# Trunk of two token mixers: product formed in place, one broadcast and the last scalings moved, one square root dropped, four splits held back

## The chip, the cores and the metric

The kernel runs on one core of one Trainium2 chip. The metric is the device time of one execution in microseconds (us), as the median of several executions. TensorE does the matrix products, VectorE and ScalarE the work on their results, GpSimd a few sums and all roots, and SyncE issues every DMA.

## What is computed

Two residual layers over 2048 positions of 1024 channels, float32. Layer 0 mixes tokens by a gated short convolution, layer 1 by causal window means; each is followed by a gated embedding, and one RMSNorm ends the trunk.

```python
def short_conv_mixer(h, w_in, w_conv, w_out):
    b_g, c_g, v, z = jnp.split(h @ w_in, 4, axis=-1)
    y = b_g * causal_conv3(c_g * v, w_conv)
    return (jax.nn.silu(z) * y) @ w_out
...
    h = x
    for i in range(DEPTH):
        hn = rmsnorm(h, norm_mix[i])
        h = h + (short_conv_mixer if i == 0 else pool_mixer)(hn, ...)
        gate = jax.nn.sigmoid(rmsnorm(h, ple_norm[i]) @ ple_w_gate[i])
        h = h + gate * (p[i] @ ple_w_proj[i])
    return rmsnorm(h, final_norm)
```

In the convolution mixer, c_g * v is called u in the kernel and in this text.

## The kernel before

Activations lie with channels on the 128 partitions and positions along the free axis, in four chunks of T = 512 positions; a first and a second pass (`sc` = 0, 1) take two chunks each. Weights come in granules of 128 x 1024. Every float32 value is split into a rounded part (ScalarE, L117 for weights, L304 and L310 for activations) and a rest (VectorE, L118, L305 and L311), and each product is three matmuls (L276 to L278); a granule of eight blocks against one chunk is 24 matmuls. The rounded weights lie in a ring of four buffers (`wring`), so a cast L117 waits until TensorE has read an older granule for the last time. PSUM has seven buffers for products and one for sums.

`mixer_a` goes through eight pairs (j = 0 to 7) of a "cv" and a "zb" step. The two chunks are multiplied together by Strassen's scheme with seven products, x11, x21, t2, t1, t3, x22 and t4, each of 12 matmuls, and three of its sums leave PSUM by a copy on ScalarE (L432) into a work tile of the pool `wk` (ten buffers). `added` (L435) makes a further tile of 512 columns. u is formed in L491 to L497 in another `wk` tile of 528 columns, whose first two columns hold the halo of the convolution.

Norms: `fin1` sums the squares across partitions on TensorE (`tot`, L344), takes the root on GpSimd (L355) and writes a diagonal `dg` (VectorE, L360); `fin2` broadcasts it with one matmul (`bc`, L365) and copies it to `rb` in SBUF (L367). A list `hooks` holds such calls; `dense_w` pops one after the 24 matmuls of a granule. In `gate`, a granule's product is scaled by `rb` (L775), passed through the sigmoid (L776), multiplied (L777) and added (L778); the square for the next norm is taken by L331 and added to `acc` (L334).

"The turn" is the end of the first pass: `gate` of layer 1 on chunk 1, then a `filler` (small products, copied out by L758) and the second pass's `mixer_a`. During both gates `ahead` lets one operand of the second pass be fetched from HBM (tile `n`, four buffers, shared with the embeddings that the gate fetches) and split, once for each k.

`gate_last` does the last gate in halves of 256 columns. After a half's last granule `finish` takes the half's norm (`fin_fast`, L369 to L386) and scales six of eight tiles on VectorE (L848), two on GpSimd (L846), and issues the output.

The program is written in one order; the compiler's scheduler then sets the order of the instructions on each engine from its own model of times, and each engine runs its list strictly in order. So a change of buffers or of a call's place can move instructions far from the lines that were edited.

Of the kernel before, what the change touches and what calls it, by code (L numbers as in the profile page):

```python
# [13 lines left out]
ALU = mybir.AluOpType  # L14
# [4 lines left out]
T = 512  # L19
# [30 lines left out]
def trunk_kernel(ctx: ExitStack, tc: tile.TileContext, xT, xN, pT, wts, par, out):  # L50
# [15 lines left out]
    def wtile():  # L66
        return wk.tile([P, 528], F32, tag="wk", name="wk")
# [365 lines left out]
        return c  # L433

    def added(ps, c):  # L435
        o = wtile()[:, :T]
        nc.vector.tensor_tensor(out=o, in0=ps, in1=c, op=ALU.add)  # L437
        return o

    def pair_steps(sc, i, X):  # L440

        pa, pb = psum(), psum()
        w = next_granule(("sum", (sc, i, 0)))
        product(pa, w, 0, X("x11"), True)
        product(pb, w, HK, X("x21"), True)
        c1 = copied(pa)
        m1 = added(pb, c1)
        yield
        w = next_granule(("sum", (sc, i, 1)))
        product(pa, w, HK, X("t2"), False)  # L450
        c2 = copied(pa)
        pc = psum()
        product(pc, w, 0, X("t1"), True)
        c5 = copied(pc)
        yield
        w = next_granule(("sum", (sc, i, 2)))
        product(pa, w, 0, X("t3"), False)
        n2 = added(pa, c5)
        product(pc, w, HK, X("x22"), False)
        m2 = added(pc, c2)  # L460
        w = next_granule(("sum", (sc, i, 3)))
        product(pa, w, 0, X("t4"), False)
        yield m1, m2, pa, n2
# [7 lines left out]
    def mixer_a(sc, X, Y, later):  # L471
        def steps(j, i):
            return pair_steps(sc, 2 * j + i, X)

        cv_steps = steps(0, 0)
        due = []
        for j in range(KT):
            zb_steps = steps(j, 1)
            if j == 0:
                next(cv_steps)  # L480
                next(zb_steps)
                look[0] = LOOK
                if sc == 0:
                    rb = list(row_stats(0))[-1]
                    rb2 = []
                    for t in range(2):
                        rb2.append(rbp.tile([P, T], F32, tag="rb", name="rb2"))
                        nc.scalar.activation(out=rb2[t], in_=rb[t], func=AF.Square)
            cs1, cs2, v1, v2 = pair_of(cv_steps)
            us = []  # L490
            for t, (c, v) in enumerate(((cs1, v1), (cs2, v2))):  # L491
                u = wtile()
                if sc == 0:
                    vec(c, c, rb2[t], ALU.mult)
                nc.gpsimd.tensor_copy(out=u[:, 0:2], in_=uh[:, j, :] if t == 0 else us[0][:, T:T + 2])
                nc.vector.tensor_tensor(out=u[:, 2:2 + T], in0=v, in1=c, op=ALU.mult)
                us.append(u)  # L497
            if sc == 0:
                nc.gpsimd.tensor_copy(out=uh[:, j, :], in_=us[1][:, T:T + 2])
            if j:  # L500
                next(zb_steps)
            next(zb_steps)
            cvs = []
            for u in us:
                cv = wtile()
                nc.scalar.activation(out=cv[:, :T], in_=u[:, 0:T], func=AF.Copy, scale=pcol(C_CONV + j))  # L506
                for t in (1, 2):
                    nc.vector.scalar_tensor_tensor(out=cv[:, :T], in0=u[:, t:t + T],  # L508
                                                   scalar=pcol(C_CONV + 8 * t + j),
                                                   in1=cv[:, :T], op0=ALU.mult, op1=ALU.add)  # L510
                cvs.append(cv)
            for args in due:
                Y.add(*args)
            due = []
            if j == KT - 1:
                Y.begin(later)
            z1, z2, b1, b2 = pair_of(zb_steps)
            if sc == 0 and FOLDS <= j + 1 < FOLDS + 4:
                fold(j + 1 - FOLDS)
            if j + 1 < KT:  # L520
                cv_steps = steps(j + 1, 0)
                next(cv_steps)
            for i in () if sc else ((), (0,), (1,), (2,), (3,), (4, 5), (6, 7), ())[j]:
                prepare_sums(*divmod(i, KT // 2))
            for t, (z, b) in enumerate(((z1, b1), (z2, b2))):
                cv = cvs[t][:, :T]
                if sc == 0:
                    vec(z, z, rb[t], ALU.mult)
                    vec(cv, cv, rb[t], ALU.mult)
                zs = wtile()[:, :T]  # L530
                nc.scalar.activation(out=zs, in_=z, func=AF.Sigmoid)
                nc.vector.tensor_tensor(out=zs, in0=z, in1=zs, op=ALU.mult)
                nc.vector.tensor_tensor(out=cv, in0=cv, in1=zs, op=ALU.mult)
                if j % 2 == t == 0:
                    yt = [acts.tile([P, 2, T], F32, tag="act", name="y") for _ in range(2)]
                nc.vector.tensor_tensor(out=yt[t][:, j % 2, :], in0=b, in1=cv, op=ALU.mult)
            if j % 2:
                due.append((j // 2, yt))
        for args in due:
            Y.add(*args)  # L540
# [26 lines left out]
    def vec(out, in0, in1, op):  # L567
        nc.vector.tensor_tensor(out=out, in0=in0, in1=in1, op=op)
# [145 lines left out]
    def mixer_out(layer, Y, src):  # L714
# [12 lines left out]
        for n, name in enumerate(OUT_NAMES):  # L727
# [16 lines left out]
                           "t3": (0, 2 * i + 1, True), "x21": (1, 2 * i, True), "t4": (1, 2 * i + 1, True)}[name])  # L744
            if name == "x21":
                s[0].fin1()
        s[0].fin2()
        return a, hs, s

    def ple_half(layer, ch, pt, wp, h):  # L750
# [66 lines left out]
        return [s.fin1, nop, last]  # L817

    def gate_last(layer, ch, a, hs, s_in):
        hooks.extend([s_in.fin1, s_in.fin2])  # L820
        pt = next_granule(("p", layer * NCH + ch))
        base = W_GATE[layer]
        half = T // 2
        ss = [Stat(half), Stat(half)]
        held, ws, wps = [], {}, {}
        seq = []
        for i in range(KT + LAG):
            if i < KT:
# [1 line left out]
            if i >= LAG:  # L830
                seq.append((i - LAG, 1))

        def finish(hf):
            c0, c1 = hf * half, (hf + 1) * half
            on_pool = (1, 3)
            for k in on_pool:
                nc.scalar.activation(out=hs[k][:, c0:c1], in_=hs[k][:, c0:c1], func=AF.Copy, scale=pcol(G_FIN + k))
            bc = ss[hf].fin_fast()
            rb = rbp.tile([P, T], F32, tag="rb", name="rb")
            nc.scalar.copy(out=rb[:, :half], in_=bc)  # L840
            for q in range(2):
                o = acts.tile([P, 4, half], F32, tag="act", name="o")
                for i in range(4):
# [12 lines left out]
        for k, hf in seq:  # L856
# [8 lines left out]
            for kk, h2, g_ps, p_ps in held:  # L865
                b0, b1 = h2 * half, (h2 + 1) * half
                gate_out(g_ps, p_ps, hs[kk], s_in.rb, b0, b1)
                ss[h2].add(hs[kk][:, b0:b1], nc.vector)
                if kk == KT - 1:
                    finish(h2)  # L870
            held = []


    warm = pst.tile([P, T], F32, tag="st", name="warm")
# [61 lines left out]
    for sc in range(2):  # L936
# [2 lines left out]
        mixer_a(sc, X, Y, xT[chs[1]])  # L939
        filler(*((0, 3) if sc else (1, 0)))  # L940
        a, hs, s = mixer_out(0, Y, xT[chs[0]])
        hooks.extend([s[1].fin1, nop, s[1].fin2])
        ab, ss = ([], []), []
        for t, ch in enumerate(chs):
            def after_gate(k):
# [8 lines left out]
        Y = Outputs(2 * sc + 1, (3, 2, 1, 0))  # L954
        mixer_b(ab, ss, Y, sc, nop if sc else between_b, h_dram[chs[1]])
        a, hs, s = mixer_out(1, Y, h_dram[chs[0]])
        hooks.extend([s[1].fin1, nop, s[1].fin2])
        if sc == 0:
            X = Operands(second_operand)

        def ahead(k):
            if sc == 0:
                X.ahead(1)

        for t, ch in enumerate(chs):
# [65 lines left out]
```

## Time and profile before

| | |
|---|---|
| median of three executions | 1821.08 us (1820.91 to 1826.33) |
| profiled execution, its own time | 1822.86 us |
| its span, first to last instruction | 1820.9 us |
| TensorE's mean granted clock | 0.991 of full speed |
| matmuls | 7998 |

A wait of an engine is given with what ended it ("<-" and the engine, tile and line of the instruction that released it). The time outside the span (1822.86 against 1820.9) is start and end of the execution.

### The profile page before, as it was taken

Reading aid. Unit: us, or ns where it says so; the run is one execution under the profiler, and the core shown is the slowest. Engines: PE = TensorE matmul, PEld = TensorE weight load, DVE = VectorE, ACT = ScalarE, POOL = GpSimd, SP = SyncE. Lnnn points to the kernel's source line nnn. Section 1 sums busy time; section 2 is a strip of 40 time slices with the busy share of each in tenths; the row PEclk is TensorE's granted clock in tenths of the full one; section 3 lists DMA queues with packets and bytes.
Section 4 is the critical chain, followed back from the end, with each engine's and each line's share of the span. In section 5 each row is a group of like instructions: output and inputs, shape, how many; then the busy total and the mean of one; then the engine's idle time right before and its main releaser. Section 6 shows DMA issues by size and latency. Waiting matters only on the chain.

```text
span 1820.9 us, 22137 instructions
## 1 busy us (share of the span) xinstructions
PE 1766.7 (97%) x7998; PEld 1457.0 (80%) x7998; DVE 1368.1 (75%) x1897; ACT 758.0 (42%) x1148; POOL 226.9 (12%) x217
## 2 busy tenths in 40 slices
PE   8899999999999999999989999999999999999996
PEld 6688888878788888887868788887878888888786
DVE  6887777987987778888876555557798766578865
ACT  6633333355654311455553333334555411145432
POOL 0100000001322000023210000000132200002310
PEclk9899999999999999999999999999999999999998
DMA  9455566895455556844673424347545522274421
GB/s 350 171 185 197 196 232 213 287 335 181 141 190 184 184 192 227 287 147 142 197 258 130 141 97 150 110 147 283 194 134 192 182 100 93 99 263 148 134 103 47
DMA packets 123934, 329.71 MB, mean 181 GB/s; under 512 B 13744, under 2 KB 15792, under 8 KB 123824
## 3 DMA queue, kind: packets, MB, share of 16 engines
q1 hardware_dynamic: 123824, 328.30, 52.0%
q8 instruction: 62, 1.02, 0.2%
q14 instruction: 48, 0.39, 0.1%
HBM read 230.73 MB, written 97.52 MB: 180 GB/s over the span
## 4 chain that ended last, share of the span: by engine, by line
PE 72%; DVE 14%; DMA 5%; issue 5%; ACT 3%; POOL 1%; SPq 0%; DVEq 0%; ACTq 0%; POOLq 0%
PE mm L276 24%; PE mm L277 24%; PE mm L278 24%; DVE w L118 3%; DVE act L305 2%; DVE act L311 2%; DMA raw<-in_wts_dram 2%; ACT w L117 2%; DMA n<-ndr 2%; DVE h L722 1%; POOL r L355 1%; DVE wk L777 1%; DVE h L808 1%; DVE dg L360 0%; DVE h L574 0%
## 5 line engine op out<-in xcount | busy, mean ns | idle before, releaser
L276 PE MATMUL mm<-act,w 128*128 128x512 f32 (+1 forms) x2432 | 932.6, 386 | 15.9 <-ACT wk L432 11.3
L277 PE MATMUL mm<-act,w 128*128 128x512 f32 (+1 forms) x2432 | 937.0, 385 | 5.9 <-DVE act L305 3.9
L278 PE MATMUL mm<-act,w 128*128 128x512 f32 (+1 forms) x2432 | 927.4, 385 | 0.5 <-DVE w L118 0.5
L276 PEld LDWEIGHTS mm<-act,w 128*128 128x128 f32 x2432 | 458.6, 189 | 115.8 <-ACT wk L432 16.9
L277 PEld LDWEIGHTS mm<-act,w 128*128 128x128 f32 x2432 | 458.2, 188 | 98.5 <-DVE act L305 5.8
L278 PEld LDWEIGHTS mm<-act,w 128*128 128x128 f32 x2432 | 458.1, 188 | 91.7 <-DVE w L118 1.0
L117 ACT CAST w<-raw 128x1024 fp32r<-128x1024 f32 (+1 forms) x291 | 289.2, 1002 | 525.4 <-PE mm L278 427.1
L118 DVE TENSOR_TENSOR w<-raw,w 128x1024 fp32r<-128x1024 f32 (+1 forms) x291 | 346.7, 1197 | 101.4 <-ACT w L117 98.5
L334 POOL TENSOR_TENSOR acc<-acc,wk 128x512 f32<-128x512 f32 x97 | 143.6, 1480 | 484.7 <-ACT wk L331 484.7
L437 DVE TENSOR_TENSOR wk<-mm,wk 128x512 f32<-128x512 f32 x96 | 66.1, 689 | 91.2 <-PE mm L278 87.2
L311 DVE SCALAR_TENSOR_TENSOR act<-h,par_sb,act 128x512 fp32r<-128x512 f32 x108 | 112.8, 1048 | 25.5 <-ACT act L310 24.8
L331 ACT ACTIVATE wk<-h 128x512 f32<-128x512 f32 (+1 forms) x119 | 71.2, 599 | 92.5 <-DVE h L778 92.5
L310 ACT ACTIVATE act<-h,par_sb 128x512 fp32r<-128x512 f32 x108 | 77.1, 719 | 75.9 <-DVE h L722 72.8
L722 DVE TENSOR_TENSOR h<-mm,h 128x512 f32<-128x512 f32 x112 | 76.0, 685 | 26.4 <-PE mm L278 24.2
L305 DVE TENSOR_TENSOR act<-n,act 128x512 fp32r<-128x512 f32 x112 | 78.9, 731 | 21.9 <-ACT act L304 21.9
L304 ACT CAST act<-n 128x512 fp32r<-128x512 f32 x112 | 65.8, 619 | 62.1 <-DMA n<-ydr 34.2
L432 ACT COPY wk<-mm 128x512 f32<-128x512 f32 x96 | 53.1, 589 | 84.2 <-PE mm L278 83.6
L508 DVE SCALAR_TENSOR_TENSOR wk<-wk,par_sb 128x512 f32<-128x512 f32 x64 | 44.1, 748 | 39.5 <-ACT wk L506 39.5
L692 DVE TENSOR_TENSOR wk<-wk 128x526 f32<-128x526 f32 (+5 forms) x80 | 55.5, 694 | 2.4
L276 PE MATMUL mm<-w 128*128 128x512 f32 (+1 forms) x144 | 48.8, 350 | 7.0 <-ACT wk L758 4.5
L776 ACT ACTIVATE wk<-wk 128x512 f32<-128x512 f32 (+1 forms) x72 | 41.3, 579 | 26.3 <-DVE wk L775 26.0
L707 ACT ACTIVATE wk<-wk 128x512 f32<-128x512 f32 x32 | 20.2, 631 | 76.8 <-DVE wk L705 76.7
(122 smaller groups left out, 1271.8 us busy)
## 6 DMA issues: line engine op xcount, KB each, us to landing
raw<-in_wts_dram SPq DMA_DIRECT2D x156, 512.0 KB, 3.4
n<-ydr SPq DMA_DIRECT2D x84, 256.0 KB, 4.5
ydr<-y SPq DMA_DIRECT2D x32, 512.0 KB, 2.9
raw<-in_wts_dram SPq DMA_DIRECT2D x64, 256.0 KB, 3.1
raw<-sdo SPq DMA_DIRECT2D x32, 512.0 KB, 5.6
raw<-sda SPq DMA_DIRECT2D x32, 512.0 KB, 3.9
pdr<-wk SPq DMA_DIRECT2D x56, 256.0 KB, 5.6
n<-pdr SPq DMA_DIRECT2D x56, 256.0 KB, 3.5
```

The costliest lines, as they stand in the source:

```text
L117: nc.scalar.copy(out=hi[:, c], in_=raw[:, c])
L118: eng.tensor_tensor(out=lo[:, c], in0=raw[:, c], in1=hi[:, c].bitcast(F32), op=ALU.subtract)
L276: nc.tensor.matmul(out=ps, lhsT=wh, rhs=ah, start=first, stop=False, skip_group_check=skip)
L277: nc.tensor.matmul(out=ps, lhsT=wh, rhs=al, start=False, stop=False, skip_group_check=skip)
L278: nc.tensor.matmul(out=ps, lhsT=wl, rhs=ah, start=False, stop=last, skip_group_check=skip)
L305: nc.vector.tensor_tensor(out=a[:, 1, :], in0=y, in1=a[:, 0, :].bitcast(F32), op=ALU.subtract)
L310: nc.scalar.activation(out=a[:, 0, :], in_=h, func=AF.Copy, scale=pcol(gcol))
L311: nc.vector.scalar_tensor_tensor(out=a[:, 1, :], in0=h, scalar=pcol(gcol), in1=a[:, 0, :].bitcast(F32), op0=ALU.mult, op1=ALU.subtract)
L331: nc.scalar.activation(out=sq, in_=h, func=AF.Square)
L334: (eng or nc.gpsimd).tensor_tensor(out=acc, in0=acc, in1=sq, op=ALU.add)
L437: nc.vector.tensor_tensor(out=o, in0=ps, in1=c, op=ALU.add)
L722: nc.vector.tensor_tensor(out=hs[t][k], in0=ps, in1=hs[t][k], op=ALU.add)
```

## The change

Five edits. (1) `added` returns a tile of 528 columns whose data begin at column 2, and u is written over c in place, so the tile u is gone: 16 work tiles for each pass. (2) `mixer_out` no longer calls `s[0].fin2()` itself, but puts it at the head of the hooks, ahead of `s[1].fin1`, so that both come one granule of the gate later. (3) `gate_last` no longer repeats `fin1` and `fin2` of its input's norm, which the gate before it has got already. (4) `finish` is parted into `root` and `finish`; both scalings are written behind the loop, and the first half's reads `rb` in SBUF where it read `bc` in PSUM. (5) For the second chunk at the turn, `ahead` makes an operand for every other k: 12 early splits in place of 16.

```diff
     def added(ps, c):
-        o = wtile()[:, :T]
-        nc.vector.tensor_tensor(out=o, in0=ps, in1=c, op=ALU.add)
+        o = wtile()
+        nc.vector.tensor_tensor(out=o[:, 2:2 + T], in0=ps, in1=c, op=ALU.add)
         return o
...
             for t, (c, v) in enumerate(((cs1, v1), (cs2, v2))):
-                u = wtile()
+                cc = c[:, 2:2 + T]
                 if sc == 0:
-                    vec(c, c, rb2[t], ALU.mult)
-                nc.gpsimd.tensor_copy(out=u[:, 0:2], in_=uh[:, j, :] if t == 0 else us[0][:, T:T + 2])
-                nc.vector.tensor_tensor(out=u[:, 2:2 + T], in0=v, in1=c, op=ALU.mult)
-                us.append(u)
+                    vec(cc, cc, rb2[t], ALU.mult)
+                nc.gpsimd.tensor_copy(out=c[:, 0:2], in_=uh[:, j, :] if t == 0 else us[0][:, T:T + 2])
+                nc.vector.tensor_tensor(out=cc, in0=v, in1=cc, op=ALU.mult)
+                us.append(c)
...
             if name == "x21":
                 s[0].fin1()
-        s[0].fin2()
+        hooks.extend([s[0].fin2, s[1].fin1, nop, s[1].fin2])
         return a, hs, s
...
     def gate_last(layer, ch, a, hs, s_in):
-        hooks.extend([s_in.fin1, s_in.fin2])
         pt = next_granule(("p", layer * NCH + ch))
...
-        def finish(hf):
+        on_pool = (1, 3)
+
+        def root(hf):
             c0, c1 = hf * half, (hf + 1) * half
-            on_pool = (1, 3)
             for k in on_pool:
                 nc.scalar.activation(out=hs[k][:, c0:c1], in_=hs[k][:, c0:c1], func=AF.Copy, scale=pcol(G_FIN + k))
             bc = ss[hf].fin_fast()
             rb = rbp.tile([P, T], F32, tag="rb", name="rb")
             nc.scalar.copy(out=rb[:, :half], in_=bc)
+            return bc, rb
+
+        def finish(hf, bc, rb):
+            c0, c1 = hf * half, (hf + 1) * half
             for q in range(2):
...
                 if kk == KT - 1:
-                    finish(h2)
+                    roots.append(root(h2))
             held = []
+        finish(0, roots[0][1][:, :half], roots[0][1])
+        finish(1, *roots[1])
...
         a, hs, s = mixer_out(1, Y, h_dram[chs[0]])
-        hooks.extend([s[1].fin1, nop, s[1].fin2])
...
         def ahead(k):
-            if sc == 0:
+            if sc == 0 and (t == 0 or k % 2):
                 X.ahead(1)
```

What the scheduler makes of it is seen in the order of each engine. Tile numbers change with the change, and lines behind L495 move by one to five.

**First pass, ScalarE, before** (the third row is the cast at 148 us of the trace). mm_1266 and mm_1318 are the two PSUM sums that are copied out; w_1301 is a granule that is needed later, and its cast waits for its place in the ring.

```order
L117 CAST w_1242<-raw_1168 128x1024
L117 CAST w_1268<-raw_1170 128x512
L117 CAST w_1301<-raw_1299 128x1024
L432 COPY wk_1295<-mm_1266 128x512
L432 COPY wk_1316<-mm_1266 128x512
L432 COPY wk_1331<-mm_1318 128x512
```

The same place in the changed kernel (mm_1260 is mm_1266, w_1262 and w_1295 are w_1268 and w_1301).

```order
L117 CAST w_1238<-raw_1164 128x1024
L432 COPY wk_1289<-mm_1260 128x512
L117 CAST w_1262<-raw_1166 128x512
L117 CAST w_1295<-raw_1293 128x1024
L432 COPY wk_1310<-mm_1260 128x512
L432 COPY wk_1325<-mm_1312 128x512
```

The first copy has moved ahead of two casts; the second and third stand where they stood.

**The turn, ScalarE, before.** wk_7751 is the gate's last product (k = 7); n_8017, n_8022 and n_8041 are fetched operands of the second pass; the last row is the filler's first copy out of PSUM.

```order
L304 CAST act_8014<-n_8012 128x512
L776 ACTIVATE wk_7751<-wk_7751 128x512
L117 CAST w_7771<-raw_7769 128x1024
L304 CAST act_8019<-n_8017 128x512
L304 CAST act_8024<-n_8022 128x512
L304 CAST act_8043<-n_8041 128x512
L331 ACTIVATE wk_7756<-h_6161 128x512
L758 COPY wk_7781<-mm_7774 128x512
```

The same place in the changed kernel; wk_7715 is the product of k = 7.

```order
L304 CAST act_7959<-n_7957 128x512
L331 ACTIVATE wk_7680<-h_6145 128x512
L304 CAST act_7964<-n_7962 128x512
L304 CAST act_7969<-n_7967 128x512
L777 ACTIVATE wk_7715<-wk_7715 128x512
L117 CAST w_7735<-raw_7733 128x1024
L304 CAST act_7993<-n_7991 128x512
L331 ACTIVATE wk_7720<-h_6145 128x512
L759 COPY wk_7745<-mm_7738 128x512
```

Between the last sigmoid and the first copy stands one cast of a fetched operand in place of three; two more stand ahead of the sigmoid.

**The end, VectorE, before.** tot, dg and bc with 145 and 146 in their numbers belong to the first half; wk_14758 is the last granule of the second half.

```order
L376 TENSOR_SCALAR ms_14587<-tot_14584 128x2
L775 TENSOR_TENSOR wk_14719<-mm_14688,rb_14275 128x256
L334 TENSOR_TENSOR acc_14014<-acc_14014,wk_14685 128x256
L381 TENSOR_TENSOR dg_14591<-ident2_92,r_14589 128x256
L777 TENSOR_TENSOR wk_14719<-mm_14688,wk_14719 128x256
L778 TENSOR_TENSOR h_12849<-h_12849,wk_14719 128x256
L775 TENSOR_TENSOR wk_14758<-mm_14727,rb_14275 128x256
L848 SCALAR_TENSOR_TENSOR o_14597<-h_12843,par_sb_90,bc_14593 128x256
L848 SCALAR_TENSOR_TENSOR o_14597<-h_12845,par_sb_90,bc_14593 128x256
L848 SCALAR_TENSOR_TENSOR o_14603<-h_12847,par_sb_90,bc_14593 128x256 x2
L848 SCALAR_TENSOR_TENSOR o_14603<-h_12849,par_sb_90,bc_14593 128x256 x2
L334 TENSOR_TENSOR acc_14014<-acc_14014,wk_14724 128x256
```

The same place in the changed kernel, up to the last granule's product wk_14690.

```order
L376 TENSOR_SCALAR ms_14532<-tot_14529 128x2
L334 TENSOR_TENSOR acc_13982<-acc_13982,wk_14617 128x256
L381 TENSOR_TENSOR dg_14536<-ident2_92,r_14534 128x256
L776 TENSOR_TENSOR wk_14651<-mm_14620,rb_13807 128x256
L778 TENSOR_TENSOR wk_14651<-mm_14620,wk_14651 128x256
L779 TENSOR_TENSOR h_12817<-h_12817,wk_14651 128x256
L334 TENSOR_TENSOR acc_13982<-acc_13982,wk_14656 128x256
L853 SCALAR_TENSOR_TENSOR o_14713<-h_12811,par_sb_90,rb_14540 128x256
L853 SCALAR_TENSOR_TENSOR o_14713<-h_12813,par_sb_90,rb_14540 128x256
L853 SCALAR_TENSOR_TENSOR o_14719<-h_12815,par_sb_90,rb_14540 128x256 x2
L853 SCALAR_TENSOR_TENSOR o_14719<-h_12817,par_sb_90,rb_14540 128x256 x2
L776 TENSOR_TENSOR wk_14690<-mm_14659,rb_13807 128x256
```

The first half's root has moved up by about one granule; the six scalings of the first half still stand ahead of the second half's root, and now ahead of the last granule's product too.

## Rows read from the trace of the kernel before

**Rows 1.** The page, busy time, share and instructions of each engine.

```profile
PE 1766.7 (97%) x7998; PEld 1457.0 (80%) x7998; DVE 1368.1 (75%) x1897; ACT 758.0 (42%) x1148; POOL 226.9 (12%) x217
```

**Rows 2.** Waits of TensorE: total us, times, longest us.

```profile
PE mm L276 <- ACT wk L432: 11.3, 12, 1.8
PE tot L373 <- DVE acc L334: 5.0, 1, 5.0
PE bc L365 <- DVE dg L360: 4.6, 4, 1.1
PE mm L276 <- ACT wk L758: 4.5, 1, 4.5
PE mm L276 <- ACT w L117: 4.0, 9, 0.7
...
PE mm L276 <- DVE wk L775: 2.4, 1, 2.4
```

**Rows 3.** Timeline, first pass, ScalarE and TensorE: start, duration, instruction, idle before.

```profile
148.16 1.05 ACT L117 CAST w<-raw 128x1024 fp32r<-128x1024 f32 x1 [3.64 <-PE mm L278]
149.12 0.58 ACT L432 COPY wk<-mm 128x512 f32<-128x512 f32 x1
...
149.75 0.50 PE L276 MATMUL mm<-act,w 128*128 128x512 f32 x1 [0.94 <-ACT wk L432]
...
153.43 0.50 PE L276 MATMUL mm<-act,w 128*128 128x512 f32 x1 [0.68 <-ACT wk L432]
...
373.73 0.50 PE L276 MATMUL mm<-act,w 128*128 128x512 f32 x1 [1.85 <-ACT wk L432]
```

**Rows 4.** Timeline, second pass, ScalarE and TensorE.

```profile
1004.36 1.05 ACT L117 CAST w<-raw 128x1024 fp32r<-128x1024 f32 x1 [3.64 <-PE mm L278]
...
1005.45 0.50 PE L276 MATMUL mm<-act,w 128*128 128x512 f32 x1 [0.46 <-ACT w L117]
...
1239.78 0.50 PE L276 MATMUL mm<-act,w 128*128 128x512 f32 x1 [1.62 <-ACT wk L432]
```

**Rows 5.** Timeline, first gate of the first pass, TensorE.

```profile
476.43 0.39 PE L278 MATMUL mm<-act,w 128*128 128x512 f32 x1
477.96 0.47 PE L365 MATMUL bc<-dg,ones_r 128*128 128x512 f32 x1 [1.14 <-DVE dg L360]
```

**Rows 6.** Timeline, the turn, VectorE and TensorE.

```profile
891.12 0.69 DVE L305 TENSOR_TENSOR act<-n,act 128x512 fp32r<-128x512 f32 x1 [2.24 <-ACT act L304]
...
929.03 0.68 DVE L775 TENSOR_TENSOR wk<-mm,rb 128x512 f32<-128x512 f32 x1
...
929.76 0.50 PE L276 MATMUL mm<-w 128*128 128x512 f32 x1 [2.44 <-DVE wk L775]
...
935.94 0.80 PE L276 MATMUL mm<-w 128*128 128x512 f32 x1 [4.52 <-ACT wk L758]
```

**Rows 7.** The chain that ended last, 925 to 945 us.

```profile
930.94 3.31 DMA n<-ndr
...
939.37 0.23 PE mm L278
```

**Rows 8.** Busy time of each engine by stretch, then TensorE's granted clock, DMA, GB/s.

```profile
936.00:938.80 2.80, 2.80 (x7) 2.23 (x8) 0.90 (x2) 2.80 (x6) 0.85 (x1) 0.50 0.93 301
```

**Rows 9.** Timeline, the end, VectorE, GpSimd and TensorE.

```profile
1805.02 2.44 DVE L848 SCALAR_TENSOR_TENSOR o<-h,par_sb,bc 128x256 f32<-128x256 f32 x6
...
1805.06 1.42 POOL L846 TENSOR_TENSOR o<-h,rb 128x256 f32<-128x256 f32 x2 [1.76 <-ACT rb L840]
...
1809.55 1.01 PE L373 MATMUL tot<-ones_f,acc 128*128 128x1 f32 x4 [4.97 <-DVE acc L334]
```

**Rows 10.** Timeline, scalings of chunks 0 and 2, VectorE and GpSimd.

```profile
906.93 6.44 DVE L808 SCALAR_TENSOR_TENSOR h<-h,par_sb,rb 128x512 f32<-128x512 f32 x8
...
907.82 1.68 POOL L334 TENSOR_TENSOR acc<-acc,wk 128x512 f32<-128x512 f32 x1 [2.69 <-ACT wk L331]
...
1763.23 5.38 DVE L808 SCALAR_TENSOR_TENSOR h<-h,par_sb,rb 128x512 f32<-128x512 f32 x8
```

More of the change, by code (lines that the diff above doesn't have):

```diff
@@ L457, in pair_steps @@
         product(pa, w, 0, X("t3"), False)
-        n2 = added(pa, c5)
+        n2 = added(pa, c5)[:, 2:2 + T]
         product(pc, w, HK, X("x22"), False)
@@ L517, in mixer_a @@
             z1, z2, b1, b2 = pair_of(zb_steps)
+            z1, z2 = z1[:, 2:2 + T], z2[:, 2:2 + T]
             if sc == 0 and FOLDS <= j + 1 < FOLDS + 4:
@@ L824, in gate_last @@
         ss = [Stat(half), Stat(half)]
-        held, ws, wps = [], {}, {}
+        held, ws, wps, roots = [], {}, {}, []
         seq = []
@@ L956, in trunk_kernel @@
         a, hs, s = mixer_out(1, Y, h_dram[chs[0]])
-        hooks.extend([s[1].fin1, nop, s[1].fin2])
         if sc == 0:
```

## The prediction, made before the changed kernel had run

> **What bounds the kernel now.** I read the page first: TensorE is busy 97% of the span [rows 1], and no other engine comes near. So an edit can only pay by removing matmuls, by removing one of TensorE's waits, or by shortening the few microseconds at the end in which TensorE has nothing left. The table of its waits [rows 2] is therefore the whole budget, and the rows listed there make up 31.8 us. Next I looked each of them up in the timeline, and then looked in the order of the changed kernel for what now stands between the waiting matmul and its releaser.
>
> **In the first pass** the picture repeats [rows 3]. The cast at 148.16 starts only when TensorE has left a granule; the PSUM copy stands behind it on ScalarE, starts at 149.12, and TensorE waits 0.94 us for it. The sum had been ready long before; the copy is late because of what is ahead of it. Twelve matmuls later comes a wait of 0.68 of another kind: the copy at its end needs the matmul just before it, nothing is late, there is only nothing else to do. Such a pair of waits is there five times; in the last (373.73) the first wait is 1.85. The line of L432 in [rows 2] adds up as 4 x 0.94 + 1.85 + 5 x 0.68 and the last one of the second pass, 1.62 + 0.67.
>
> **In the second pass** TensorE waits six times 0.46 us (the first at 1005.45) for a cast that can start only when the old granule is left [rows 4], and once 1.62 at 1239.78 as above.
>
> **At the turn** VectorE is late: the last product L775 comes at 929.03, the wait before it is 2.44, and a second of 4.52 follows [rows 6]. The chain of work [rows 7] puts most of the second on a fetch of an operand (3.31 us from the issue), whose cast stands on ScalarE ahead of the copy that TensorE waits for. [...]
>
> **The change part by part.**
>
> *u in place of c.* It takes no instruction away: copies, casts and multiplications stay, only 32 tiles go. Its effect is the order. In the changed order the first copy stands ahead of the two casts at all five places, and nothing that it needs comes later than the matmuls long done: 4 x 0.94 + 1.85 = 5.6 us. The 0.68 stays where t2 and t3 still follow each other (three places); at the first and the last place 10 or 11 other matmuls now stand between, so 2 x 0.68 = 1.4. First pass: 7.0 us, between 5.6 and 8.4 (all five).
>
> In the second pass TensorE's order is altogether new. Where the first use of a new granule came 3 matmuls behind the last use of the old one, it now comes at least 25 later, 25 x 0.23 [rows 7] = 5.8 us, against 1.05 for the cast and as much for its rest: 6 x 0.46 = 2.8 goes, and the 1.62 (copy now ahead of the casts). I take off 1.0, because an order that the trace has never shown will have small waits of its own: 3.4, between 0 and 4.4. At the start of the program, one cast's wait of 0.7 (the longest in the line of L117 in [rows 2]) also falls, since 12 matmuls are put ahead of it: 0.7, between 0 and 0.7.
>
> *fin2 behind a granule.* The broadcast stood behind 15 of the first granule's 24 matmuls and waited four times 1.14 for `dg` [rows 5, 2]. Now all 24 stand ahead of it. The nine matmuls take 9 x 0.23 = 2.1 us, more than the 1.14, and the place of `dg` on VectorE is as before: 4.6 us for the four. What is late next is the first L775, by less than 1 us; it runs 6 us behind its granule there anyway, with PSUM buffers to spare, so nothing waits. Bounds 3.5 and 4.6 (one of the four lost).
>
> *One root less.* Two sums and one broadcast of 512 columns, 3 x 0.23 = 0.7 us of TensorE. Seven VectorE instructions go too, at a place where it has time.
>
> *Fewer splits at the turn.* VectorE stood 2.24 us at 891.12 for a fetched operand that is now split earlier; that and two splits (0.6 each, the pace of the rows around) no longer stand ahead of the last product: it comes 3.5 us earlier, near 925.5, before TensorE asks for its buffer at 929.76 - 2.44 = 927.3. So the 2.44 goes. TensorE then asks for the filler's first copy six matmuls later, at 928.7. On ScalarE one operand's cast still stands ahead of it. Its fetch can be issued when a buffer `n` comes free: product at 925.5, 0.6 for it, 0.6 for the first split behind it, 926.7. Then 3.3 for the fetch [rows 7], 0.6 each for cast, square and copy: 931.8. TensorE waits 3.1 in place of 4.5 + 2.4 = 7.0: 3.9 us won. The half clock cost 2.8 x 0.5 = 1.4 [rows 8]; a shorter wait may bring half of that back, 0.7. Together 4.6; bounds 2.4 (only the first wait goes) and 8.4 (both, and the clock). The four splits held back are done in the second pass, where VectorE is not pressed.
>
> *The end.* The scalings do not come behind the second root: in the changed order the six still stand ahead of the last granule's product, but the first half's root is about a granule earlier. They start some 2.3 us before 1805.02, near 1802.7, when the copy `rb` is there; six take 2.44 [rows 9]; product, sigmoid, multiplication, sum, square and addition then follow at 0.35 to 0.45 each, and the last `tot` comes near 1807.8 in place of 1809.55: 1.8 us. But these scalings now read two operands in SBUF while GpSimd starts its two multiplications (1.42 us) at the same moment. The nearest row for that is the scaling of chunk 0: eight took 6.44 beside one addition of GpSimd, and 5.38 without one [rows 10]; so 1.0 comes off, and 0.8 us is left, between 0.2 and 1.8. [...]
>
> The sum: 7.0 + 3.4 + 0.7 + 4.6 + 0.7 + 4.6 + 0.8 = 21.8 us. The profiled execution took 1822.86 in all, so its successor would take 1801.1; the median shown is 1.8 lower, which gives 1799.3. I say **1800**.
>
> **The rivals.**
>
> *A: the new order of the second pass brings its own waits.* If its copies land where those of the first pass were, each of seven pairs gets 0.94 + 0.68 = 1.6, 11.3 us in all. For it: that a wait of 0.94 came only from a copy one place too late in a list [rows 3]. Against it: in the order the copies stand ahead of the casts there. Time: 1811.
>
> *B: only the edits made by hand pay.* The order changes, but each wait that goes returns at the next matmul, as where ScalarE and VectorE are only just in time. Then broadcasts 4.6, root 0.7 and the turn's first wait 2.4 are left, 7.7 in all: 1813.
>
> *C, slower: the second pass becomes bound by ScalarE's list.* Its order was made by a model of times and not by this chip. If a copy stands behind a cast that waits for the ring at each of its 16 steps, and a contiguous t2 and t3 follow, 16 x 1.6 = 25.9 us come on top, and the 3.4 are lost: 1800 + 29.3 = 1829. It is slower by over 0.3% only from 15 of 16 steps on, since 0.3% above the median is 1826.5. Against it: before, just one step of that pass showed such a pair of waits [rows 4].
>
> *D: nothing moves*, because the turn's wait only goes to the next fetch and the removed waits come back in equal number: within 5.5 us of 1821.
>
> **How the numbers follow.** About 0.3%, 5.5 us, is what a measurement of this kernel can tell from no change; faster means below 1815.6. My forecast has 0.62 (its own range, 1794 to 1806, takes the bounds of the turn and of the second pass), A 0.14, B 0.14, C 0.04, D 0.06. A and nearly all of B (0.12) lie below the mark with the forecast: faster 0.88; D and the rest of B: same 0.08; slower 0.04. The range takes in A and B and the upper bounds of all terms but the rarest: 1793 to 1814.
>
> **What would show it.** In the waits of TensorE: L432 down from 11.3 to about 3 (three of 0.68 and one of 0.67); L365 gone; L117 from 4.0 to about 1; no L775; the filler's copy between 1 and 4.5; the last `tot` after a wait near 4 us. 7995 matmuls. [...] The prediction is wrong if new lines stand in that table with more than 5 us in sum (A, C, or B by many small ones), if the broadcast still waits, or if the filler's copy waits longer than 4.5 us, because the three splits that now stand ahead of the last sigmoid each meet a late fetch.

## The result, and the profile after

The changed kernel takes 1802.03 us by median (four runs, 1794.94 to 1803.02) against 1822.15 for the kernel before (1820.91 to 1826.33): a ratio of 0.988, 95% interval 0.986 to 0.990. Repeated without any change beside other kernels (x8_control below), it took 1798.27 against 1821.87: 0.987, 0.986 to 0.988. The gain is 20 to 24 us, and 1800 was predicted.

The profiled execution is the 1794.94 one, with a span of 1793.2; it lies 7 to 8 us below the three others, so the stages below are read from two traces, this one and that of the repeat (span 1795.4).

TensorE in the page of the changed kernel, against [rows 1]: three matmuls less, and 98% busy.

```profile
PE 1756.5 (98%) x7995; PEld 1455.2 (81%) x7995; DVE 1363.5 (76%) x1890; ACT 758.6 (42%) x1146; POOL 229.2 (13%) x216
```

Its waits, to be held against [rows 2] (total us, times, longest us). The product's line has moved from L775 to L776, the filler's copy from L758 to L759.

```profile
PE tot L373 <- DVE acc L334: 5.4, 1, 5.4
PE tot L344 <- ACT rb L367: 3.9, 4, 1.0
PE mm L276 <- ACT wk L432: 3.2, 5, 0.7
...
PE mm L276 <- ACT wk L759: 2.7, 2, 1.8
PE bc L365 <- DVE dg L360: 2.7, 2, 1.6
...
PE mm L276 <- ACT w L117: 0.6, 2, 0.4
```

L432 has gone from 11.3 to 3.2, the casts L117 from 4.0 to 0.6, the wait for the product is no longer there. One row is new: the sums `tot` wait four times 1.0 for `rb`. And `bc` still waits, twice in place of four times.

To see where the time came from, I took the start of the n-th matmul of TensorE's list from the timeline of each trace. The columns give how much earlier it starts than before; from 7800 on, n is counted without the three matmuls that edit 3 removes, and the last line compares the spans.

| n | starts before at | stage that ends here | changed | repeat | x2 | x6 | x10 |
|---|---|---|---|---|---|---|---|
| 400 | 110.79 | start | 3.9 | 1.9 | -0.4 | 3.0 | 3.4 |
| 1800 | 420.40 | first pass | 12.2 | 10.9 | 0.3 | 12.1 | 12.5 |
| 4000 | 924.44 | gates | 11.6 | 11.1 | 0.2 | 12.6 | 12.6 |
| 4200 | 978.77 | turn | 17.2 | 16.1 | 3.5 | 20.5 | 18.9 |
| 5600 | 1303.66 | second pass | 23.8 | 22.6 | 3.5 | 27.1 | 25.5 |
| 7200 | 1668.42 | gates | 24.2 | 23.0 | 3.9 | 27.6 | 25.9 |
| 7800 | 1779.57 | last gate | 27.3 | 25.1 | 6.2 | 30.1 | 28.6 |
| span | 1820.9 | end | 27.7 | 25.5 | 6.6 | 30.5 | 31.9 |

The kernel gains in the two passes and at the turn. In the gates, where the four broadcasts were to bring 4.6, it gains next to nothing. These columns are the gain of one execution over another: the spans give 27.7 and 25.5 where the medians give 20.1 and 23.6, so 2 to 8 us of them are no property of the kernels.

### The profile page after: what moved, and what is told of

It is laid out like the page before. It is cut to its first block, busy times and chain, and to the rows that moved or that the text cites. A ratio compares the mean times of both kernels' runs of the same rounds, so it can differ in the third digit from the quotient of the medians.

```text
span 1793.2 us, 22178 instructions
## 1 busy us (share of the span) xinstructions
PE 1756.5 (98%) x7995; PEld 1455.2 (81%) x7995; DVE 1363.5 (76%) x1890; ACT 758.6 (42%) x1146; POOL 229.2 (13%) x216
## 4 chain that ended last, share of the span: by engine, by line
PE 76%; DVE 13%; DMA 5%; issue 3%; ACT 2%; POOL 1%; DVEq 0%; SPq 0%; ACTq 0%; POOLq 0%
PE mm L276 25%; PE mm L277 25%; PE mm L278 25%; DVE w L118 3%; DVE act L311 2%; DVE act L305 2%; DMA n<-ndr 1%; DMA sdo<-n 1%; DVE h L723 1%; ACT w L117 1%; DMA n<-in_wts_dram 1%; DMA raw<-in_wts_dram 1%; DVE wk L778 0%; DVE dg L360 0%; POOL r L355 0%
## 5 line engine op out<-in xcount | busy, mean ns | idle before, releaser
L117 ACT CAST w<-raw 128x1024 fp32r<-128x1024 f32 (+1 forms) x291 | 290.2, 1002 | 503.9 <-PE mm L278 343.1
L334 POOL TENSOR_TENSOR acc<-acc,wk 128x512 f32<-128x512 f32 x97 | 139.0, 1433 | 472.5 <-ACT wk L331 472.4
L331 ACT ACTIVATE wk<-h 128x512 f32<-128x512 f32 (+1 forms) x119 | 71.3, 599 | 101.9 <-DVE h L779 101.9
L305 DVE TENSOR_TENSOR act<-n,act 128x512 fp32r<-128x512 f32 x112 | 78.0, 723 | 19.6 <-ACT act L304 19.2
L432 ACT COPY wk<-mm 128x512 f32<-128x512 f32 x96 | 54.8, 587 | 83.5 <-PE mm L278 80.8
L706 DVE TENSOR_TENSOR wk<-mm,rb 128x512 f32<-128x512 f32 x32 | 22.0, 688 | 37.5 <-PE mm L278 37.5
```

Of the source, the lines that this page charges most:

```text
L117: nc.scalar.copy(out=hi[:, c], in_=raw[:, c])
L305: nc.vector.tensor_tensor(out=a[:, 1, :], in0=y, in1=a[:, 0, :].bitcast(F32), op=ALU.subtract)
L331: nc.scalar.activation(out=sq, in_=h, func=AF.Square)
L334: (eng or nc.gpsimd).tensor_tensor(out=acc, in0=acc, in1=sq, op=ALU.add)
```

## The experiments

My theory after the result: u in place gives nearly all; the later broadcast gives its gain back through the one PSUM buffer that `tot` and `bc` share; the turn's rest is the filler's copies behind casts of fetched operands; the end is held by six scalings slowed by GpSimd (3.51 us beside its two multiplications, in before 2.44). The rivals: that the edits made by hand carry the gain, and that the later broadcast is worth its 4.6 and something else ate it. Ratios are to the kernel before, on the same chip.

**x1_u_only**: before, with edit 1 alone.

```diff
-        o = wtile()[:, :T]
+        o = wtile()
```

> The kernel before with u formed in place of c and nothing else. Theory: this edit alone carries most of the gain through the order it gives, because the copies out of PSUM (L432) now stand ahead of the casts that wait for the ring: the waits of TensorE for L432 fall from 11.3 us to about 3, those for the cast L117 from 4.0 to about 1, and the time is 15 to 18 us below that of before, near 1805. Rival: the new order only shifts waits, and the gain came from the edits made by hand; then the time is within 6 us of before, 1816 or more.

1801.58 against 1820.88: 0.990 (0.988 to 0.991), 19.3 us. Its waits:

```profile
PE mm L276 <- ACT wk L759: 4.6, 1, 4.6
PE bc L365 <- DVE dg L360: 4.5, 4, 1.1
...
PE mm L276 <- ACT wk L432: 2.7, 4, 0.7
...
PE mm L276 <- DVE wk L776: 1.7, 1, 1.7
```

L432 is down as in the changed kernel, `bc` and the turn wait as before. In its trace the lead grows by 9.1 us in the first pass and by 6.6 in the second, as in the changed kernel, and by 0.3 at the turn. One edit, which takes no instruction away, brings nearly the whole gain.

**x2_all_but_u**: the changed kernel with the tile u back.

```diff
-                us.append(c)
+                us.append(u)
```

> The changed kernel with u in a tile of its own again; the other four edits stay. Theory: the waits for L432 are back at about 11 us and those for L117 at about 4, and only the turn (about 6), the root (0.7) and the end (0.7) pay, less about 2 for the broadcast: 1815 to 1818. Rival (the edits made by hand carry the gain): 1808 or less.

1815.84: 0.997 (0.996 to 0.998), 5.0 us. L432 is back at 10.6 (12 times), L117 at 4.0 (9 times); and `tot` waits four times 1.0 for `rb` here too, with none of edit 1. So that wait belongs to edit 2. 19.3 and 5.0 add up to 24.3, against 20.1 and 23.6 measured for both together.

**x3_all_but_fin2**: the changed kernel with edit 2 undone.

```diff
-        hooks.extend([s[0].fin2, s[1].fin1, nop, s[1].fin2])
+        s[0].fin2()
```

> The changed kernel with the broadcast of mixer_out where it was before; the other four edits stay. Theory: as made, this edit loses: the four waits of 1.1 before the broadcast come back (4.6 us), but the four of 1.0 of the sum that follows it for the copy rb (3.9) and two of the second broadcast (2.7) go, so the time is 1 to 3 us below that of the changed kernel. Rival, my prediction's own term: the edit wins 4.6 us, and without it the time is 4 to 5 us above that of the changed kernel.

1797.60: 0.987 (0.985 to 0.988). `bc` waits 4.5 in four times again, and no sum waits for `rb`. Against the repeat (1798.27) there is no difference that these times can show: neither the 4.6 of the prediction nor the loss of 1 to 3 that I had expected here.

**x4_fin2_nop**: one more granule between the broadcast and the next sum.

```diff
-        hooks.extend([s[0].fin2, s[1].fin1, nop, s[1].fin2])
+        hooks.extend([s[0].fin2, nop, s[1].fin1, nop, s[1].fin2])
```

> The changed kernel with one more empty granule between the broadcast of the first chunk and the sum of the second. Theory: the sum waits only because it comes one granule behind the broadcast, while the copy rb stands on ScalarE behind the rounding of acc and a cast of weights; one granule later the four waits of 1.0 are gone, and 3 to 4 us are won against the changed kernel. Rival: the wait moves on, since the second broadcast then comes before its dg is ready, with four waits of 1 to 2 us in the table, and the time is that of the changed kernel.

1800.09: 0.989 (0.988 to 0.990). The sums no longer wait for `rb`, and the time has gone to another row of its waits:

```profile
PE bc L365 <- DVE dg L360: 8.7, 4, 4.4
```

The wait can be moved, not removed, by the order of the hooks: with the sum later, the second broadcast waits up to 4.4 us.

**x8_control**: the changed kernel as it is.

> The changed kernel once more, unaltered, on the chip of the three runs beside it, since its first four executions spread over 8 us. Theory: the spread is that of fetches from HBM at the start and at the turn, whose waits differ between two traces of the same order, while the stages between take the same time to 0.1 us: median 1798 to 1803, and the stage from the first mixer to the turn as in the first trace. Rival: there is a difference in every stage (a clock or a memory that is slower throughout).

1798.27 (1797.19 to 1799.70): 0.987 (0.986 to 0.988). Its trace is the column "repeat" above. Beside the changed kernel's first trace, the start (2.0 us) and the last gate (1.1) differ, the first pass, its gates and the turn by 0.7 each. Only the second pass, its gates and the end agree to 0.1 us, which I had expected of every stage but the start and the turn.

**x5_turn_only**: before, with edit 5 alone.

```diff
-            if sc == 0:
+            if sc == 0 and (t == 0 or k % 2):
```

> The kernel before with four splits held back at the turn and nothing else. Theory: VectorE's last product of the gate comes 4 to 6 us earlier, the wait of 2.4 us goes, the second shrinks to between 1 and 3, and a wait of 1 to 3 us for the filler's later copies is new, since they stand behind casts of fetched operands: 3 to 5 us below before, 1816 to 1818. Rival: the splits held back are missed in the second pass, whose waits for L305 grow, and the time is that of before.

1817.12 (1813.9 to 1823.7): 0.998 (0.997 to 0.999), 4.75 us. By the medians fewer splits pay by themselves what the turn was predicted to. Its trace puts 3.2 us of its gain at the turn and 2.5 in the last gate, which this edit leaves as it was.

**x6_copies_first**: at the turn, ScalarE's casts of the second pass's fetched operands may only be issued behind the filler's last copy out of PSUM.

```diff
-            nc.scalar.copy(out=e, in_=ps)
+            copied_at[0] = nc.scalar.copy(out=e, in_=ps)
...
+        with tc.issue_after(turn_at[0].ins):
+            return split_act(n)
```

> The changed kernel with the casts of the second pass's operands, those not made during the gates, queued on ScalarE behind the filler's last copy. Theory: at the turn the copies are late only for the casts of fetched operands that stand ahead of them; the two waits for L759 (2.7 us in sum) fall below 0.5, and the time falls by 2 to 4 us against the unaltered run beside it. Rival: the casts are then late for the second pass itself, with waits of TensorE for L305 of the same size, and the time stays.

1793.47 (1792.19 to 1794.07): 0.984 (0.983 to 0.985), 4.8 us less than the repeat. ScalarE's timeline at the turn of this kernel (here the copy is L764 and the cast L305):

```profile
914.21 2.02 ACT L764 COPY wk<-mm 128x512 f32<-128x512 f32 x4
...
919.36 2.04 ACT L764 COPY wk<-mm 128x512 f32<-128x512 f32 x4
921.26 0.62 ACT L433 COPY wk<-mm 128x512 f32<-128x512 f32 x1
921.74 2.21 ACT L305 CAST act<-n 128x512 fp32r<-128x512 f32 x4
```

Both groups of copies stand ahead of the casts, and no row of TensorE's waits names L764. Two windows, of the changed kernel and then of x6 (length, busy time of TensorE, its weight loads, VectorE, ScalarE, GpSimd; granted clock, DMA, GB/s):

```profile
910.00:960.00 50.00, 47.26 (x208) 38.42 (x207) 41.17 (x58) 28.39 (x46) 5.87 (x6) 1.00 0.75 252
```

```profile
910.00:960.00 50.00, 49.62 (x217) 40.46 (x216) 37.30 (x54) 29.74 (x48) 6.13 (x6) 1.00 0.74 246
```

TensorE is busy 49.62 of 50 us. So the two waits for copies go when the casts stand behind the copies; with the casts, VectorE's splits come later too, and the run does not part the two. Not all of the 4.8 us are from here: in the table the turn gains 7.9 in place of the repeat's 4.9, 3.0 more, and another 1.1 comes from the start, which this edit leaves as it was. The rival holds in part, for fetches still come late, only further down the list. In this trace TensorE waits 0.16 for such a cast, in x10 below, with the same order, 1.19 (ScalarE, then TensorE, of x10):

```profile
947.24 0.62 ACT L305 CAST act<-n 128x512 fp32r<-128x512 f32 x1 [2.98 <-DMA n<-ndr]
...
947.91 0.50 PE L277 MATMUL mm<-act,w 128*128 128x512 f32 x1 [1.19 <-ACT act L305]
```

In x11 and x9 the same wait is 1.48 and 2.12.

**x7_tail_behind**: the first half's scalings are held behind two VectorE instructions of the second half's root, two channels behind `ms` and the rest behind `dg`.

```diff
-        finish(0, roots[0][1][:, :half], roots[0][1])
+        for q, at in enumerate((ss[1].ms_at, ss[1].dg_at)):
+            with tc.issue_after(at.ins):
+                finish(0, roots[0][1][:, :half], roots[0][1], (q,))
```

> The changed kernel with the first half's scalings queued on VectorE behind the second half's root: two between the mean square and the diagonal, four behind the diagonal, where VectorE stood 0.8 and 1.8 us. Theory: the last granule's product no longer stands behind six scalings (3.5 us), and the last sum comes 2.7 us earlier; the scalings fit in the idle time; the end of the program comes 2 to 2.7 us earlier. Rival: beside GpSimd's power the scalings, which read two operands in SBUF, hold it up (or are held up) by about 1 us, and only 1 to 1.7 us are won.

1795.91: 0.985 (0.984 to 0.987), 2.4 us less than the repeat by median, with overlapping intervals. From matmul 7800 to the end its trace gains 3.3 us on before, that of the changed kernel 0.4. The last rows of x7's timeline, TensorE and VectorE:

```profile
1782.70 0.61 PE L373 MATMUL tot<-ones_f,acc 128*128 128x1 f32 x4 [2.79 <-DVE acc L334]
...
1783.43 0.87 DVE L853 SCALAR_TENSOR_TENSOR o<-h,par_sb,rb 128x256 f32<-128x256 f32 x2
...
1784.83 1.67 DVE L853 SCALAR_TENSOR_TENSOR o<-h,par_sb,rb 128x256 f32<-128x256 f32 x4
```

The last sum waits 2.79 in place of 5.42, a difference of 2.6. The six scalings now take 0.87 + 1.67 = 2.54, inside the wait for the second root. The rival, that GpSimd's power costs 1 us of the gain, is not borne out.

**x10_copies_tail**: x6 and x7 together.

> The changed kernel with both moves: the filler's copies ahead of the casts of fetched operands, and the first half's scalings behind the second half's root. Theory: the two are at different places and add up: 4.8 and 2.4 us below the unaltered changed kernel (1798.3), so near 1791. Rival: what is won at the turn is partly lost at the end or in the second pass, 1793 or more.

1791.85 (1790.65 to 1793.87): 0.984 (0.983 to 0.985). **x9_best** is the same with edit 2 undone (the diff of x3).

> The kernel of the run before it with the broadcast of mixer_out back where it was before the change. Theory: four waits of 1.1 for dg come back (4.5 us), and four of 1.0 for the copy rb (3.9) and two of the second broadcast (1.4 to 2.7) go: 1 to 2 us below the run before it, near 1789.5. Rival, my prediction's own term: the edit is worth up to 4.6 us, and the time is above that of the run before it.

1791.40 (1789.18 to 1793.75): 0.983 (0.982 to 0.985). The two can't be told apart, so once more the times show no worth of edit 2, and the 1 to 2 us that I had expected of its removal are not seen; in x9 `bc` waits 4.6 in four times, in x10 `tot` 3.9 in four times and `bc` 2.1 in two. Both beat the changed kernel, and the kernel before by 30 us.

**x11_root_twice**: x10 with the second root of edit 3 back.

```diff
     def gate_last(layer, ch, a, hs, s_in):
+        hooks.extend([s_in.fin1, s_in.fin2])
```

> The kernel of the first run of this call with the last gate's second root put back. Theory: three matmuls of 512 columns, 0.7 us, and nothing else on the path: 0.5 to 1.5 us above that run. Rival: the seven VectorE instructions and the wait for the second rb delay the last gate's products too, and 2 us or more come on top.

1794.36: 0.985 (0.984 to 0.987), 2.5 us more than x10 by median, with overlapping intervals. The row of the first half's `ms` on VectorE, in x10 and then in x11:

```profile
1769.25 0.16 DVE L377 TENSOR_SCALAR ms<-tot 128x2 f32<-128x2 f32 x1 [0.35 <-PE tot L374]
```

```profile
1776.58 0.16 DVE L377 TENSOR_SCALAR ms<-tot 128x2 f32<-128x2 f32 x1 [2.83 <-PE tot L374]
```

With the repeated root the first half's sum comes late, as in the kernel before:

```profile
1802.37 0.16 DVE L376 TENSOR_SCALAR ms<-tot 128x2 f32<-128x2 f32 x1 [2.83 <-PE tot L373]
```

From matmul 7800 to the end, x10 gains 3.3 us on the kernel before and x11 1.5; in the last gate it is 2.6 and 2.1. So the second root costs 2.4 in these traces, more than the 0.5 to 1.5 expected. The two spans differ by 4.9, since x11 also gains 1.7 less at the turn, with the same order there.

**x12_all_ahead**: x10 with all 16 splits early again, so without edit 5.

```diff
-            if sc == 0 and (t == 0 or k % 2):
+            if sc == 0:
```

> The kernel of the first run of this call with an operand made ahead for every k again (16 splits in place of 12). Theory: with the copies ahead of the casts, the splits still delay VectorE's last product of the gate, and a wait for it (L775 before) of 1.5 to 3 us comes back: 2 to 3 us above that run. Rival: the number of splits did not matter, only that casts stood ahead of the copies; then the time is that of the run within 1 us.

1794.24: 0.985 (0.984 to 0.986), 2.4 more than x10 by median, with overlapping intervals. TensorE waits once more at the turn, for a copy:

```profile
919.63 0.50 PE L277 MATMUL mm<-w 128*128 128x512 f32 x1 [1.66 <-ACT wk L764]
```

But between the matmuls 4000 and 4200 its trace gains 6.6 on before, and that of x10 6.3: the last product comes late (915.59, in x10 910.78), and the wait of 1.19 for a late fetch that x10 has is not there. Whether the number of splits still matters once the copies stand first stays open.

## Why the prediction was right, step by step

**The two passes: the mechanism right, the size too small.** Terms 7.0 and 3.4; the table has 8.3 and 9.0, and 6.6 twice. The waits that were to go went, the ones that were to stay stayed (L432: four of 0.7, and in the first trace one of 0.5 that was to go), and none came in their place, so that the 1.0 taken off for them in the second pass was not needed. The rest is how a wait is counted. TensorE in the timeline of the changed kernel, at one that stayed:

```profile
191.27 0.39 PE L278 MATMUL mm<-act,w 128*128 128x512 f32 x1
192.34 0.50 PE L276 MATMUL mm<-act,w 128*128 128x512 f32 x1 [0.68 <-ACT wk L432]
192.67 0.39 PE L277 MATMUL mm<-act,w 128*128 128x512 f32 x1
```

The idle time of 0.68 is counted from the modelled end of the matmul before it, 0.39 behind its start, though the matmuls ahead of it follow each other every 0.23 (nine steps from 189.23 to 191.27); and the matmul behind the wait comes 0.33 later, not 0.23. Undisturbed, the third row would have stood at 191.27 + 2 x 0.23 = 191.73; it stands 0.94 later. Each such wait costs 0.26 more than it shows; the 18 waits of the two passes in the trace of before, worked out in the same way, give 0.27. Seven were to go in the first pass, 7.0 + 7 x 0.26 = 8.8, and seven in the second, 4.4 + 1.8 = 6.2: both near the table. I had summed a column that leaves out a quarter of a microsecond per row.

**The broadcasts: the step that failed.** The sentence was "What is late next is the first L775 ... so nothing waits", worth 4.6. What is late next is the sum. Behind the moved broadcast stands `s[1].fin1` one granule later, and its `tot` needs the PSUM buffer that the copy `rb` empties. The timeline of the changed kernel there, ScalarE and TensorE:

```profile
471.72 0.62 ACT L339 CAST acc_hi<-acc 128x512 fp32r<-128x512 f32 x1 [2.03 <-DVE acc L334]
...
472.24 1.04 ACT L117 CAST w<-raw 128x1024 fp32r<-128x1024 f32 x1
...
473.19 0.58 ACT L367 COPY rb<-bc 128x512 f32<-128x512 f32 x1
...
473.82 0.50 PE L344 MATMUL tot<-acc_hi,ones_r 128*128 128x512 f32 x1 [1.00 <-ACT rb L367]
```

The copy stands behind the rounding of `acc`, which waits 2.03 for VectorE, and behind a cast of weights. That makes 1.00, four times. Two broadcasts wait besides: 1.64 at 845.10, where `dg` (844.27) stands on VectorE behind the split of a fetched operand. Together 3.9 + 2.7 = 6.6 (in the repeat 3.9 + 1.9) for the 4.6 of [rows 2]. I had looked at the waiting engine and at the next reader of the result, and not at the next user of the buffer. By the prediction's own sign ("if the broadcast still waits") this part was wrong. The times of x3 and x9 can't tell the edit's worth from nothing; the starts of the matmuls can. At the four places where the old wait went and the sum waits instead (n from 2000 to 2300, 3500 to 3650, 5700 to 5950, 7270 to 7400), each of eight traces with edit 2 gains 0.35 to 0.47 us on before, and each of four without it (x1, x3, x5, x9) stays within 0.1 of before. Where the second broadcast waits (3650 to 3720, 7400 to 7450) the eight lose 1.9 to 3.2 in sum, and the four nothing. So edit 2 loses 0.2 to 1.5 us, 0.8 on average, where 4.6 were to be won.

**The turn: near in size, by another route.** 4.6 predicted; 5.6 and 4.9 in the table, 3.2 in the trace of x5 (4.75 by its median). The last product stands at 911.80, 4.3 us behind the end of its granule in place of 9.9: 5.6 earlier, where I had said 3.5. The rest of the wait I had put at 3.1 in one piece; it is 0.93 and 1.81. For each, the rows show ScalarE ahead of it and then TensorE:

```profile
915.97 0.62 ACT L304 CAST act<-n 128x512 fp32r<-128x512 f32 x1 [0.71 <-DMA n<-ndr]
916.81 0.63 ACT L331 ACTIVATE wk<-h 128x512 f32<-128x512 f32 x1 [0.22 <-DVE h L779]
...
917.96 0.50 PE L276 MATMUL mm<-w 128*128 128x512 f32 x1 [0.93 <-ACT wk L759]
...
926.59 1.95 ACT L304 CAST act<-n 128x512 fp32r<-128x512 f32 x3 [3.24 <-DMA n<-ndr]
...
930.11 0.50 PE L276 MATMUL mm<-act,w 128*128 128x512 f32 x1 [1.81 <-ACT wk L759]
```

The second stems from casts that wait for their fetch ahead of a copy that could have run, as the prediction said of the kernel before [rows 7]; x6 confirms it by turning that order round. Ahead of the first stands such a cast too, but in this trace it is the square L331 that comes last, and it waits for VectorE; in the repeat the cast itself waits 1.58 for its fetch, and L331 follows at once. The granted clock stayed at 1.00 in both traces, so the whole 1.4 of [rows 8] came back and not half. That 1.4 was an estimate from the clock of the window; in the timeline of before a matmul comes every 0.43 us there (936.54 to 938.67) and every 0.23 behind it (938.98 to 939.67).

The size is luck in part. On ScalarE, VectorE and TensorE the order at the turn is the same in five kernels (the changed one, its repeat, x3, x4, x7), and from matmul 4000 to 4200 their traces gain 5.6, 4.9, 0.9, 5.6 and 2.1. In x3 the casts ahead of the second wait stood 4.35 us for their fetch (3.24 here), the wait was 2.91 and the clock behind it 0.50. With the copies first (x6, x10, x9, x11) the same stage gains 7.9, 6.3, 4.7 and 4.6. So the order of the copies is worth some 2 us there on average, and traces of one order differ by more than that.

**The root.** 0.7 for three matmuls, and 0.7 measured: from matmul 7600 to 7800 both traces of the changed kernel gain 0.7 on before, and x1 and x5, which keep this root, 0.0. The last gate as a whole shows 3.1 and 2.1, but most of that is no edit's: x5, which leaves this gate as it was, gains 2.5 there. The traced execution of before had waited 2.4 for `acc_hi` (a row of TensorE's waits that [rows 2] leaves out), which x5 waits 1.4 for and the changed kernel 0.6, and behind that wait its clock was at half. TensorE's row of that wait in before, and a window behind it:

```profile
1750.47 0.50 PE L344 MATMUL tot<-acc_hi,ones_r 128*128 128x512 f32 x1 [2.38 <-ACT acc_hi L339]
```

```profile
1751.20:1754.50 3.30, 3.30 (x17) 3.20 (x16) 2.03 (x5) 0.72 (x2) 0.00 (x0) 0.50 0.02 5
```

In x5 and in both traces of the changed kernel it stayed at 1.00, which gives each of them 1.5 us (from 1751.06 to 1754.58 the 16 steps took 3.5 us in before; at 0.12 for 256 columns, as ahead of its wait, and 0.23 for 512 they would have taken 2.0). And x11 shows a second use that I had credited to edit 4: without the repeated root the first half's sum is ready early, 1.8 us at the end.

**The end.** 0.8 predicted, 0.4 in the table. The order was read rightly: in the changed kernel the scalings start ahead of the last product. VectorE and GpSimd in its timeline, then TensorE's last sum:

```profile
1775.63 3.51 DVE L853 SCALAR_TENSOR_TENSOR o<-h,par_sb,rb 128x256 f32<-128x256 f32 x6 [0.54 <-ACT rb L841]
1775.68 1.60 POOL L851 TENSOR_TENSOR o<-h,rb 128x256 f32<-128x256 f32 x2 [4.06 <-ACT rb L841]
1779.06 0.41 DVE L776 TENSOR_TENSOR wk<-mm,rb 128x256 f32<-128x256 f32 x1
...
1781.81 1.01 PE L373 MATMUL tot<-ones_f,acc 128*128 128x1 f32 x4 [5.42 <-DVE acc L334]
```

Six scalings take 3.51 beside GpSimd's two multiplications. In before they took 2.44 beside the same two, but with one operand in PSUM [rows 9], and in x7, with both operands in SBUF and no multiplication of GpSimd beside them, 2.54: 1.0 lost, as was taken off. The wait for the last sum grew to 5.42, from 4.97, and only x7 and the kernels built on it put the scalings where nothing waits for them.

**The start.** 0.7 predicted; 3.9 and 1.9 in the two traces, -0.4 in x2. Eleven traces with edit 1 gain 1.8 to 3.9 there, x2 and x5 without it -0.4 and 1.1. So edit 1 gains at the start, and by the traces more than the term; the spread between traces of one kernel is 2.0, so the size stays open.

**The rivals.** A, 1811, and C, 1829: no new waits in the second pass, whose lead grows by 6.6. B, 1813, only the edits made by hand pay: the reverse of x1 and x2. D: excluded by the interval.

**The sum came out right partly because two errors cancelled**: in the two traces the passes and the turn brought about 5.5 us more than their terms, and the broadcasts, which lost 1.5 and 0.7, 6.1 and 5.3 less. That was luck and not insight.

## What to carry to other kernels

Before an edit that delays an instruction, look at the next user of every buffer that it holds, on all engines, and not only at the next reader of its result. In these traces an engine's list was run in order (at the turn the filler's copies stood behind casts that waited 3.24 us for a fetch, and TensorE waited 1.81 for the first of them), so a step that may wait for a fetch should not stand ahead of a PSUM copy that TensorE needs: at one place turning this round was worth 4.8 us by the medians, 3.0 of them seen there in the traces, and the window showed no shortage of ScalarE (28 of 50 us). The fetch itself stays late, and a later matmul may wait for it (0.16 to 2.12 us in x6, x10, x11 and x9). A change that deletes nothing but lets a scheduler find another order can be worth more than all edits made by hand, and it is read from the order of the engines, wait by wait.

## What the runs showed of the hardware that I had not expected

TensorE's granted clock fell behind some waits and not behind others. Behind a wait of 5.42 us the four small matmuls of the last sum ran at 0.50 and took 1.01 us, in x7 behind 2.79 at 1.00 and took 0.61. The windows, of the changed kernel and of x7:

```profile
1781.80:1783.00 1.20, 1.01 (x4) 0.93 (x4) 0.14 (x1) 0.00 (x0) 0.00 (x0) 0.50 0.00 0
```

```profile
1782.70:1783.50 0.80, 0.61 (x4) 0.52 (x4) 0.15 (x2) 0.00 (x0) 0.00 (x0) 1.00 0.00 0
```

At the turn, waits of 0.93 and 1.81 left it at 1.00; in x7 one of 2.95 there was followed by 0.50. But the length of the last wait alone does not decide it: the repeat's wait of 1.84 left the clock at 1.00, and in x11 it was 0.50 behind a matmul that had waited only 1.48 (948.52). Window of x11:

```profile
950.30:953.60 3.30, 3.30 (x9) 2.60 (x8) 2.56 (x4) 1.22 (x3) 0.00 (x0) 0.50 0.39 123
```

What else counts is not shown. And executions of one kernel differ by several microseconds (1794.94 to 1803.02 for the changed one). Part of that lies in the start, where two traces differ by 2.0, and part at the turn, where five traces with the same order gain between 0.9 and 5.6; the slower executions of the changed kernel itself were not traced, so how much each has is open.
